# Turning the attention weights of a latent-attention stage with DVE squares and transfers within SBUF

## The chip, the cores and the metric

One core of a Trainium2 chip runs the whole program. The metric is device time in microseconds (us), as the median of the runs of one kernel. Engines: PE multiplies matrices, DVE and ACT work on vectors, POOL is hardly used here, and SP issues the transfers (DMA). SBUF is the on-chip memory of 128 partitions; PSUM holds the accumulators, eight banks of 128 x 512 f32.

## The reference

A decoder trunk of two layers on 256 tokens of width 2048, all f32. Layer 0 mixes by a gated MLP, layer 1 by latent attention with 12 heads; beside either, 4 heads attend to 256 memory tokens, and a gated feed-forward part follows. What matters here is the mixer of layer 1:

```
def mla_attention(q_lat, g_q_lat, w_uq, w_uk, w_uv, c_kv, k_rope, cos, sin):
    q = (rmsnorm(q_lat, g_q_lat) @ w_uq).reshape(B, S, MLA_HEADS, NOPE_DIM + ROPE_DIM)
    ...
        qa = jnp.einsum('bqhn,rhn->bqhr', qn, w_uk)
        s = (jnp.einsum('bqhr,bkr->bhqk', qa, c_kv)
             + jnp.einsum('bqhp,bkp->bhqk', qr, k_rope)).astype(jnp.float32) * scale
        s = jnp.where(k_pos[None, :] <= q_pos[:, None], s, -jnp.inf)
        p = jax.nn.softmax(s, axis=-1).astype(c_kv.dtype)
        o_lat = jnp.einsum('bhqk,bkr->bqhr', p, c_kv)
        return jnp.einsum('bqhr,rhv->bqhv', o_lat, w_uv)

def memory_attention(q_m, mem, g_mem, w_mem_kv):
    s = jnp.einsum('bshd,bmhd->bhsm', q, k).astype(jnp.float32) * (MEM_HEAD_DIM ** -0.5)
    p = jax.nn.softmax(s, axis=-1).astype(v.dtype)
    return jnp.einsum('bhsm,bmhd->bshd', p, v).reshape(B, S, MEM_W)

    # in the trunk, for layer 1
    x = x + jnp.concatenate([main, mo], axis=-1) @ w_out[l]
```

Softmax runs along the keys, and the sum over the keys that follows contracts them. On the chip a matmul contracts over partitions, so the weights p, which leave softmax with queries on partitions, must be turned before they can be used.

## The kernel before

All weights lie in HBM and are read once, in chunks of 128 x 1024 f32 (512 KB; 384 KB for the queries). `chunk` takes one of four `raw` buffers, issues the load on SP, and splits the chunk into two rounded parts: ACT copies it to `whi` (L110), DVE takes the difference to `wlo` (L111). A product then is three matmuls: high by high (L147), high by the low part of the activations (L148) and low by high (L150); in `gemm_tm`, with weights as the moving operand, these are L178 to L180. Activations are held as such pairs too, made by `split` (L232 on ACT, L233 on DVE).

The stage of layer 1 that matters (`layer_b`) computes the values in three chunks of 512 columns, `values(0)` to `values(2)`, into `scratch`; then for each of six pairs of heads `queries(i)` (two chunks of w_uq), `keys(i)` (one chunk of w_uk, expanded from the latent), and `scores(h)` for both heads: a matmul of kn and qn (L865) and two for the rotary part (L867), DVE's mask and maximum (L872, a custom operation), ACT's exponential with its sum (L877), DVE's reciprocal and scaling (L882). `turn(h)` transposes the three 128x128 blocks of a head's weights on PE (L889) and ACT copies them out of PSUM (L891). `attend(h)` multiplies by the values (L898, L899) and splits the result into `mainhl`. The four memory heads go the same way in `memory_scores` (L513; maximum L519, exponential L524, scaling L529), `memory_turn` (four transposes, L537, copied out by L541) and `memory_out` (L548). The loop over the pairs is written as a software pipeline: pair i's scores come one step after its queries, its turn and attend two steps after.

`w_out` is the output projection, 16 blocks of rows in chunks of two and in pairs of chunks, over eight such sweeps; the memory heads' rows come first. Its hooks run other work behind a given chunk of its first sweep.

Work of all engines is written in one program order; outside regions that fix it (`manual_schedule`) a scheduler reorders each engine's instructions by its own estimates, and each engine then takes its list in that order. A transfer issued by an engine waits in that engine's list until its source is ready, and all behind it waits too.

Later in the program, the feed-forward part has two operations that also occur in the change: DVE transposes of 32x32 squares (L968, `slot` from `xT`), and transfers within SBUF on SP in pieces of 32 elements (L973, `xt` from `slot`).

Of the kernel before, what the change touches and what calls it, by code (L numbers as in the profile page):

```python
# [8 lines left out]
F32 = mybir.dt.float32  # L9
# [3 lines left out]
AF = mybir.ActivationFunctionType  # L13
ALU = mybir.AluOpType
AX = mybir.AxisListType

P = 128
D = 2048
S = 256
NB = D // P  # L20
GH = 12
GW = GH * 128
MH = 4
# [45 lines left out]
    return out  # L69


class Kernel:
    def __init__(self, ctx, tc, t, out):
        self.tc, self.nc, self.t, self.out = tc, tc.nc, t, out
        self.ctx = ctx
        self.n = 0
        pool = lambda name, bufs=1, **k: ctx.enter_context(tc.tile_pool(name=name, bufs=bufs, **k))
# [16 lines left out]
    def chunk(self, src, nk, ncol, gains=None, twice=False, place=PLACE):  # L94
        nc, n = self.nc, nk * ncol
        raw = self.wp.tile([P, 1024], F32, tag="raw", name=self.uid("raw"), bufs=4)
        hi = self.wp.tile([P, 1088], F32R, tag="whi", name=self.uid("whi"), bufs=4)
        lo = self.wp.tile([P, 1088], F32R, tag="wlo", name=self.uid("wlo"), bufs=4)
        hi, lo = (x[:, place : place + 1024] for x in (hi, lo))
        view = lambda x: x[:, :n].rearrange("p (k c) -> p k c", k=nk)  # L100
        nc.sync.dma_start(out=view(raw), in_=src)
        if twice:
            both = hi[:, : 2 * n].rearrange("p (k o c) -> p k o c", o=2, c=ncol)
            for k in range(nk):
                r, h = view(raw)[:, k, :], both[:, k, 0, :]
                nc.scalar.activation(h, r, AF.Copy, scale=gains[k])
                nc.vector.scalar_tensor_tensor(both[:, k, 1, :], r, gains[k], h.bitcast(F32), ALU.mult, ALU.subtract)
            return hi[:, : 2 * n].rearrange("p (k c) -> p k c", k=nk)
        if gains is None:
            nc.scalar.activation(hi[:, :n], raw[:, :n], AF.Copy)  # L110
            nc.vector.tensor_tensor(lo[:, :n], raw[:, :n], hi[:, :n].bitcast(F32), ALU.subtract)  # L111
# [397 lines left out]
    def memory_scores(self, l, h, q, pool):  # L509
        nc = self.nc  # L510
        acc = self.psum()
        for sb in range(2):
            nc.tensor.matmul(  # L513
                acc[:, sb * S : (sb + 1) * S], q[:, sb * P : (sb + 1) * P], self.kT[l][:, h, :], start=True, stop=True
            )
        scale = 128 ** -0.5
        a3 = acc.rearrange("p (a m) -> p a m", a=2)
        mx = self.tmp(pool, [P, 2], "mx", 4)
        nc.vector.tensor_reduce(mx, a3, AX.X, ALU.max)  # L519
        nc.vector.tensor_scalar(mx, mx, -scale, None, ALU.mult)  # L520
        p = self.tmp(pool, [P, 2, S], "mp", 2)
        den = self.tmp(pool, [P, 2], "den", 4)
        for sb in range(2):
            nc.scalar.activation(  # L524
                p[:, sb, :], a3[:, sb, :], AF.Exp, bias=mx[:, sb : sb + 1], scale=scale, accum_out=den[:, sb : sb + 1]
            )
        nc.vector.reciprocal(den, den)
        for sb in range(2):
            nc.vector.tensor_scalar(p[:, sb, :], p[:, sb, :], den[:, sb : sb + 1], None, ALU.mult)  # L529
        return p  # L530

    def memory_turn(self, p, pool, bufs=2):
        nc = self.nc
        acc = self.psum()
        for mb in range(2):
            for sb in range(2):
                nc.tensor.transpose(  # L537
                    acc[:, mb * S + sb * P : mb * S + (sb + 1) * P], p[:, sb, mb * P : (mb + 1) * P], self.ident
                )
# [195 lines left out]
    def layer_b(self):  # L735
# [9 lines left out]
        with tc.tile_pool(name="lb", bufs=1) as lb:  # L745
# [103 lines left out]
            def keys(pr):  # L849
                kn[pr] = self.tmp(lp, [P, 2, S], "kn", 2)  # L850

                def ev(b, acc):
                    nc.scalar.activation(kn[pr][:, b : b + 2, :], acc, AF.Copy)

                self.gemm_fm(self.rows(wuk, pr * 256, 256), list(range(4)), 2, lambda k: chl[:, k, :], ev, nk=4)

            def scores(h):
                pr, j = divmod(h, 2)
                sc = self.psum()
                part = (slice(0, P), slice(P, 3 * P))  # L860
                for qb in range(2):
                    n = P * (qb + 1)
                    o = sc[:, part[qb]]
                    q = slice(qb * P, (qb + 1) * P)
                    mm(o, qn[pr][:, j, q], kn[pr][:, j, :n], start=True, stop=False)  # L865
# [4 lines left out]
                p = self.tmp(lp, [P, 3 * P], "p", 3)  # L870
                for qb in range(2):
                    nc.vector.tensor_tensor_reduce(  # L872
                        p[:, part[qb]], sc[:, part[qb]], self.mask[:, part[qb]], 1.0, -3e38, ALU.add, ALU.max, mx[:, qb : qb + 1]
                    )
                nc.vector.tensor_scalar(mx, mx, -scale, None, ALU.mult)
                for qb in range(2):
                    nc.scalar.activation(  # L877
                        p[:, part[qb]], p[:, part[qb]], AF.Exp, bias=mx[:, qb : qb + 1], scale=scale, accum_out=den[:, qb : qb + 1]
                    )
                nc.vector.reciprocal(den, den)  # L880
                for qb in range(2):
                    nc.vector.tensor_scalar(p[:, part[qb]], p[:, part[qb]], den[:, qb : qb + 1], None, ALU.mult)  # L882
                pa[h] = p

            def turn(h):
                p = pa.pop(h)
                acc = self.psum()
                for i in range(3):
                    nc.tensor.transpose(acc[:, i * P : (i + 1) * P], p[:, i * P : (i + 1) * P], self.ident)  # L889
                pT = self.tmp(lp, [P, 512], "pT", 3)  # L890
                nc.scalar.activation(pT[:, : 3 * P], acc[:, : 3 * P], AF.Copy)  # L891
                pa[h] = pT

            def attend(h):
                pT = pa.pop(h)
# [3 lines left out]
                mm(o[:, P:S], v[:, 1, cols], pT[:, S : S + P], start=False, stop=True)  # L899
                self.split(hl[:, h, :], o[:, :S])  # L900

            def mscores(h):
                pm[h] = self.memory_scores(1, h, qm[:, h, :], lp)

            def mturn(h):
                pm[h] = self.memory_turn(pm[h], lp, 3)

            def mout(h):
                self.memory_out(1, h, pm.pop(h), hl)

            n = GH // 2
            for i in range(n):
                queries(i)
                keys(i)
                if i >= 2:
                    turn(2 * i - 4)
                    turn(2 * i - 3)
                if i in (2, 4):
                    values(i // 2)
                if i >= 1:  # L920
                    scores(2 * i - 2)
                    scores(2 * i - 1)
                if i >= 2:
                    attend(2 * i - 4)
                    attend(2 * i - 3)
                if i < MH:
                    mscores(i)
                if 1 <= i <= MH:
                    mturn(i - 1)
                if 2 <= i <= MH + 1:  # L930
                    mout(i - 2)
            each = lambda f, *hs: [lambda h=h: f(h) for h in hs]
            for f in each(scores, 10, 11) + each(turn, 8, 9):
                f()
            hooks = {0: each(attend, 8, 9) + each(turn, 10, 11), 2: each(attend, 10, 11)}
            self.w_out(1, hl, [12, 13, 14, 15] + list(range(12)), hooks)
            ctx.close()

    def run(self):
# [146 lines left out]
```

## Time and profile before

| | |
|---|---|
| median of 3 runs | 2047.26 us (2047.03 to 2047.42) |
| the profiled execution | 2047.1 us |
| its span in the profile | 2045.4 us |
| granted PE clock | 0.999 |
| PE busy | 2035.9 us, 16232 instructions |
| DVE busy | 1359.1 us, 1859 instructions |
| ACT busy | 1043.5 us, 1345 instructions |
| weights and inputs read from HBM | 387.88 MB, 191 GB/s |

Times in the profile count from the start of the span. A group of instructions reads: line, engine, operation, output <- inputs, sizes, count, then total and mean duration, then the idle time of the engine ahead of it and what ended that. Matmuls are pipelined, so that the durations of neighbours overlap, and the cost of one is the distance to the next one's start.

### The profile page before, as it was taken

Reading aid. Unit: us, or ns where it says so; the run is one execution under the profiler, and the core shown is the slowest. Engines: PE = TensorE matmul, PEld = TensorE weight load, DVE = VectorE, ACT = ScalarE, POOL = GpSimd, SP = SyncE. Lnnn points to the kernel's source line nnn. Section 1 sums busy time; section 2 is a strip of 40 time slices with the busy share of each in tenths; the row PEclk is TensorE's granted clock in tenths of the full one; section 3 lists DMA queues with packets and bytes.
Section 4 is the critical chain, followed back from the end, with each engine's and each line's share of the span. In section 5 each row is a group of like instructions: output and inputs, shape, how many; then the busy total and the mean of one; then the engine's idle time right before and its main releaser. Section 6 shows DMA issues by size and latency. Waiting matters only on the chain.

```text
span 2045.4 us, 39005 instructions
## 1 busy us (share of the span) xinstructions
PE 2035.9 (100%) x16232; PEld 1969.4 (96%) x16232; DVE 1359.1 (66%) x1859; ACT 1043.5 (51%) x1345; POOL 94.5 (5%) x125
## 2 busy tenths in 40 slices
PE   9999999999999999999999999999999999999998
PEld 8989999999999999999999999999988999889997
DVE  6865667767556666557689875786655667656675
ACT  6754644555435554345555665455544455434553
POOL 0000013000000000000052001300000000000000
PEclk9999999999999999999999999999999999999999
DMA  8675465666666666666666644578766666666654
GB/s 309 188 230 175 155 197 188 196 196 188 203 189 193 199 191 198 190 196 192 189 196 177 179 129 154 183 209 219 225 196 194 189 198 193 194 196 188 196 185 155
DMA packets 219858, 394.62 MB, mean 193 GB/s; under 512 B 30880, under 2 KB 37408, under 8 KB 219552
## 3 DMA queue, kind: packets, MB, share of 16 engines
q1 hardware_dynamic: 219392, 391.60, 62.6%
q8 instruction: 127, 2.08, 0.4%
q10 hardware_dynamic: 288, 0.52, 0.1%
q14 instruction: 51, 0.42, 0.1%
HBM read 387.88 MB, written 2.10 MB: 191 GB/s over the span
## 4 chain that ended last, share of the span: by engine, by line
PE 99%; DMA 0%; issue 0%; DVE 0%; ACT 0%; POOLq 0%; POOL 0%
PE ps L150 26%; PE ps L147 26%; PE ps L148 26%; PE ps L178 6%; PE ps L180 6%; PE ps L179 6%; DMA raw<-in_w_mem_kv 0%; PE ps L865 0%; PE ps L548 0%; PE ps L513 0%; PE ps L485 0%; PE ps L484 0%; PE ps L487 0%; PE ps L688 0%; PE ps L898 0%; PE ps L867 0%
## 5 line engine op out<-in xcount | busy, mean ns | idle before, releaser
L111 DVE TENSOR_TENSOR wlo<-raw,whi 128x1024 fp32r<-128x1024 f32 (+1 forms) x672 | 818.6, 1235 | 612.9 <-issue 414.6
L110 ACT ACTIVATE whi<-raw 128x1024 fp32r<-128x1024 f32 (+1 forms) x672 | 705.2, 1056 | 794.1 <-PE ps L148 591.6
L147 PE MATMUL ps<-xhl,whi 128*128 128x256 f32 x3264 | 752.8, 277 | 0.0
L148 PE MATMUL ps<-xhl,whi 128*128 128x256 f32 x3264 | 750.8, 276 | 0.0
L148 PEld LDWEIGHTS ps<-xhl,whi 128*128 128x128 f32 x3264 | 612.8, 188 | 0.4
L147 PEld LDWEIGHTS ps<-xhl,whi 128*128 128x128 f32 x3264 | 612.6, 188 | 0.4
L150 PE MATMUL ps<-xhl,wlo 128*128 128x256 f32 x3264 | 403.2, 276 | 0.0
L150 PEld LDWEIGHTS ps<-xhl,wlo 128*128 128x128 f32 x3264 | 385.1, 188 | 0.0
L147 PE MATMUL ps<-h,whi 128*128 128x256 f32 x704 | 161.6, 276 | 0.0
L148 PE MATMUL ps<-h,whi 128*128 128x256 f32 x704 | 161.5, 276 | 0.0
L603 DVE SCALAR_TENSOR_TENSOR c<-a,cT,c 128x255 f32<-128x255 f32 (+1 forms) x352 | 146.3, 478 | 0.0
L179 PE MATMUL ps<-wlo,h 128*128 128x512 f32 (+1 forms) x364 | 139.0, 382 | 0.0
L180 PE MATMUL ps<-whi,h 128*128 128x512 f32 (+1 forms) x364 | 138.7, 382 | 0.0
L178 PE MATMUL ps<-whi,h 128*128 128x512 f32 (+1 forms) x364 | 138.3, 382 | 0.0
L148 PEld LDWEIGHTS ps<-h,whi 128*128 128x128 f32 x704 | 131.9, 188 | 0.0
L147 PEld LDWEIGHTS ps<-h,whi 128*128 128x128 f32 x704 | 131.9, 188 | 0.0
L600 ACT ACTIVATE c<-a,cT 128x256 f32<-128x256 f32 x176 | 91.6, 591 | 76.5 <-DVE a L228 76.5
L147 PE MATMUL ps<-mainhl,whi 128*128 128x256 f32 x512 | 118.0, 277 | 0.0
L148 PE MATMUL ps<-mainhl,whi 128*128 128x256 f32 x512 | 117.9, 276 | 0.0
L148 PEld LDWEIGHTS ps<-mainhl,whi 128*128 128x128 f32 x512 | 96.1, 188 | 0.0
L147 PEld LDWEIGHTS ps<-mainhl,whi 128*128 128x128 f32 x512 | 96.1, 188 | 0.0
L150 PE MATMUL ps<-h,wlo 128*128 128x256 f32 x704 | 86.9, 276 | 0.0
(246 smaller groups left out, 1972.2 us busy)
## 6 DMA issues: line engine op xcount, KB each, us to landing
raw<-in_w_ffn_up SPq DMA_DIRECT2D x352, 512.0 KB, 4.3
raw<-in_w_ffn_down SPq DMA_DIRECT2D x176, 512.0 KB, 4.6
raw<-in_w_out SPq DMA_DIRECT2D x64, 512.0 KB, 4.8
raw<-in_w_in_a SPq DMA_DIRECT2D x56, 512.0 KB, 4.4
raw<-in_w_mem_kv SPq DMA_DIRECT2D x30, 512.0 KB, 5.6
raw<-in_w_in_b SPq DMA_DIRECT2D x16, 512.0 KB, 4.1
raw<-in_w_uq SPq DMA_DIRECT2D x12, 384.0 KB, 3.4
raw<-in_w_kv_a SPq DMA_DIRECT2D x8, 512.0 KB, 4.3
```

Source lines behind the costliest of these rows:

```text
L110: nc.scalar.activation(hi[:, :n], raw[:, :n], AF.Copy)
L111: nc.vector.tensor_tensor(lo[:, :n], raw[:, :n], hi[:, :n].bitcast(F32), ALU.subtract)
L147: mm(acc, wh, x[:, :S], start=first, stop=False)
L148: mm(acc, wh, x[:, S:], start=False, stop=False)
L150: mm(acc, wl, x[:, :S], start=False, stop=last)
L178: mm(acc, xh, wh, start=first, stop=False)
L179: mm(acc, xh, wl, start=False, stop=False)
L180: mm(acc, xl, wh, start=False, stop=last)
L600: nc.scalar.activation(c[:, i, :], a[:, i, :], AF.Identity, scale=w(2), bias=w(3))
L603: nc.vector.scalar_tensor_tensor(o, a[:, i, : S - 2 + j], w(j), o, ALU.mult, ALU.add)
```

## The change

In layer 1 the weights p are no longer turned on PE.

- Softmax's last scaling is done by ACT (a copy with a scale per partition) in place of DVE.
- All heads of a batch write their weights into one wide buffer: `pm` for the four memory heads, a part of `scratch` for heads 0 to 5, `room` for heads 6 to 11.
- `Turn.squares` lets DVE transpose the 32x32 squares of that buffer into a small one, regrouped so that each band of 32 columns is together. There are 2 such operations of 128 x 1024 for the memory heads and 3 of 128 x 768 for either batch of heads, 8 in all.
- `Turn.place` moves one band of 32 partitions from the small buffer to another band of the wide one, by a transfer on SP. 16 places complete a turn, 48 in all. The memory heads' places have 32 x 16 pieces of 32 elements, the others 32 x 18.
- The places are not issued where they are written: `ask` puts them in a list, and `chunk` takes the next entry off it right after a weight load (`some`), so that a stated number of places follows each load.
- Within the stage PE and SP now run in program order, and the order is another: memory scores are early; `values(1)` follows keys(3); the four memory outputs, the attends of heads 0 to 5 and `values(2)` follow scores(11); the attends of heads 6 to 11 follow the third chunk of `w_out`.

```diff
+class Pending(list):
+    def some(self):
+        for f in self.pop(0) if self else ():
+            f()
+
+    def ask(self, steps, counts):
+        for n in counts:
+            self.append(steps[:n])
+            steps = steps[n:]
...
         nc.sync.dma_start(out=view(raw), in_=src)
+        self.pending.some()
...
         for sb in range(2):
-            nc.vector.tensor_scalar(p[:, sb, :], p[:, sb, :], den[:, sb : sb + 1], None, ALU.mult)
+            if by_act:
+                nc.scalar.activation(p[:, sb], p[:, sb], AF.Copy, scale=den[:, sb : sb + 1])
+            else:
+                nc.vector.tensor_scalar(p[:, sb], p[:, sb], den[:, sb : sb + 1], None, ALU.mult)
...
+                def squares(self, first, count):
+                    src = self.p[:, first * P : (first + count) * P].rearrange("p (n b c) -> p n b c", n=count, b=4)
+                    dst = self.small[:, :, first : first + count, :].rearrange("p b n c -> p n b c")
+                    nc.vector.transpose(dst, src)
+
+                def place(self, q, b):
+                    out = self.p[lanes(b), : self.n * P].rearrange("p (n q c) -> p n q c", n=self.n, q=4)[:, :, q, :]
+                    nc.sync.dma_start(out=out, in_=self.small[lanes(q), b])
...
                 for qb in range(2):
-                    nc.vector.tensor_scalar(p[:, part[qb]], p[:, part[qb]], den[:, qb : qb + 1], None, ALU.mult)
-                pa[h] = p
-
-            def turn(h):
-                p = pa.pop(h)
-                acc = self.psum()
-                for i in range(3):
-                    nc.tensor.transpose(acc[:, i * P : (i + 1) * P], p[:, i * P : (i + 1) * P], self.ident)
-                pT = self.tmp(lp, [P, 512], "pT", 3)
-                nc.scalar.activation(pT[:, : 3 * P], acc[:, : 3 * P], AF.Copy)
-                pa[h] = pT
+                    nc.scalar.activation(p[:, part[qb]], p[:, part[qb]], AF.Copy, scale=den[:, qb : qb + 1])
...
+            with tc.manual_schedule(engines={mybir.EngineType.SP, mybir.EngineType.PE}):
+                for i in range(GH // 2):
+                    if i == 3:
+                        memory.ask(0, 0, 6, 5, 5)
+                    if i == 5:
+                        turns[0].ask(0, 0, 16)
+                    for f in (queries, keys) if i else (keys, mscores, queries):
+                        f(i)
+                    if i == 2:
+                        each(lambda j: memory.squares(8 * j, 8), *range(2))
+                    if i == 4:
+                        each(lambda j: turns[0].squares(6 * j, 6), *range(3))
+                    if i == 3:
+                        values(1)
+                    if i >= 1:
+                        each(scores, 2 * i - 2, 2 * i - 1)
+                    each(mscores, *((1,), (2, 3), (), (), (), ())[i])
+                turns[1].squares(0, 6)
+                each(scores, 10, 11)
+                each(mout, *range(MH))
+                turns[1].squares(6, 6)
+                each(attend, *range(GH // 2))
+                turns[1].squares(12, 6)
+                values(2)
+                turns[1].ask(0, 6, 6, 4)
+                self.w_out(1, hl, [12, 13, 14, 15] + list(range(12)), {2: [lambda: each(attend, *range(GH // 2, GH))]})
```

The orders below list an engine's instructions as line, operation, output <- inputs and sizes; a number behind a name tells buffers of one kind apart. SP around the second third of the values, before (raw_13708 to raw_13771 are queries(3) and keys(3)):

```order
L101 DMA raw_13708<-in_w_uq 128x2x384
L101 DMA raw_13732<-in_w_uq 128x2x384
L101 DMA raw_13771<-in_w_uk 128x4x256
L101 DMA raw_13816<-in_w_uv 128x2x512
L101 DMA raw_13834<-in_w_uv 128x2x512
L101 DMA raw_13927<-in_w_uq 128x2x384
```

And SP at the two chunks of `values(1)` after, behind queries(3) and keys(3):

```order
L114 DMA raw_13857<-in_w_uq 128x2x384
L114 DMA raw_13881<-in_w_uq 128x2x384
L114 DMA raw_13920<-in_w_uk 128x4x256
L893 DMA pm<-room 32x16x32 x6
L114 DMA raw_13959<-in_w_uv 128x2x512
L893 DMA pm<-room 32x16x32 x5
L114 DMA raw_13982<-in_w_uv 128x2x512
L893 DMA pm<-room 32x16x32 x5
L114 DMA raw_14043<-in_w_uq 128x2x384
```

Six places now stand ahead of the first w_uv chunk, five more ahead of the second. What they wait for stands on DVE after, where ps_13821 and ps_13838 are the scores of heads 2 and 3 and the square is the second of the memory heads':

```order
L913 ISA scratch,mx_13828<-ps_13821,mask 128x128
L913 ISA mx_13828 128x1
L913 ISA scratch,mx_13828<-ps_13821,mask 128x256
L913 ISA mx_13828 128x1
L913 ISA scratch,mx_13845<-ps_13838,mask 128x128
L913 ISA mx_13845 128x1
L913 ISA scratch,mx_13845<-ps_13838,mask 128x256
L913 ISA mx_13845 128x1
L889 STREAM_TRANSPOSE room<-pm 128x8x4x32
L916 TENSOR_SCALAR mx_13828<-mx_13828 128x2
```

The square is taken only when the masks and maxima of scores(2) and scores(3) are done. SP at the start of the output projection, before:

```order
L101 DMA raw_14521<-in_w_out 128x2x512
L101 DMA raw_14527<-in_w_out 128x2x512
L101 DMA raw_14603<-in_w_out 128x2x512
L101 DMA raw_14609<-in_w_out 128x2x512
L101 DMA raw_14673<-in_w_out 128x2x512
L101 DMA raw_14679<-in_w_out 128x2x512
```

And after, from the places of heads 0 to 5 (scratch<-scratch) and `values(2)` on:

```order
L893 DMA scratch<-scratch 32x18x32 x16
L114 DMA raw_14409<-in_w_uv 128x2x512
L114 DMA raw_14427<-in_w_uv 128x2x512
L114 DMA raw_14451<-in_w_out 128x2x512
L114 DMA raw_14457<-in_w_out 128x2x512
L893 DMA room<-scratch 32x18x32 x6
L114 DMA raw_14517<-in_w_out 128x2x512
L893 DMA room<-scratch 32x18x32 x6
L114 DMA raw_14529<-in_w_out 128x2x512
L893 DMA room<-scratch 32x18x32 x4
L114 DMA raw_14617<-in_w_out 128x2x512
```

The places of heads 6 to 11 (room<-scratch) stand ahead of the third, fourth and fifth chunk of w_out. In all, PE has 52 matmul instructions fewer, DVE 24 instructions fewer, ACT 16 more, and SP 48 transfers more.

More of the change, by code (lines that the diff above doesn't have):

```diff
@@ L69, in two_pi_pieces @@
     return out
+class Pending(list):
[6 more added lines that the diff above has]
+            steps = steps[n:]
+        assert not steps
 class Kernel:
@@ L908, in mout @@
             def mout(h):
[L909 to L936, printed above, removed]
+                self.memory_out(1, h, pm[:, 512 * h : 512 * (h + 1)], hl)
+            turns = [batch(k) for k in range(2)]
+            each = lambda f, *hs: [f(h) for h in hs]
+            with tc.manual_schedule(engines={mybir.EngineType.SP, mybir.EngineType.PE}):
[24 more added lines that the diff above has]
+                self.w_out(1, hl, [12, 13, 14, 15] + list(range(12)), {2: [lambda: each(attend, *range(GH // 2, GH))]})
```

41 lines of the change are left out of this document (29 added, 12 removed).

## Prediction

> **What bounds the kernel now.** I read the page first, then who waits for whom on PE, then the stage that the change rewrites.
>
> ```profile
> span 2045.4 us, 39005 instructions
> PE 2035.9 (100%) x16232; PEld 1969.4 (96%) x16232; DVE 1359.1 (66%) x1859; ACT 1043.5 (51%) x1345; POOL 94.5 (5%) x125
> PE 99%; DMA 0%; issue 0%; DVE 0%; ACT 0%; POOLq 0%; POOL 0%
> PE ps L288 <- DVE ones L279: 1.1, 1, 1.1
> PE ps L147 <- ACT whi L132: 0.4, 1, 0.4
> ```
>
> The first lines are the page's: PE is busy for the whole span and makes up 99% of the chain that ended last. The last two are the full list of PE's waits: 1.5 us, all at the start. So this kernel is the list of its matmuls: a matmul that goes is worth its own time, and a wait that comes in is paid in full. The stage in question runs from the first queries to the third chunk pair of the output projection:
>
> ```profile
> 1144.91:1247.45 102.54, 102.54 (x782) 98.28 (x781) 73.79 (x207) 70.71 (x158) 0.10 (x1) 1.00 0.46 135
> ```
>
> (Columns: length, busy PE, weight loads, DVE, ACT, POOL, granted clock, DMA share, GB/s.) 102.54 of 102.54 us is matmul; DVE and ACT have about 30 us to spare each, but spread thin.
>
> **What the change removes.** PE loses 36 transposes of attention weights (12 heads x 3) and 16 of memory weights (4 heads x 4), 52 in all.
>
> ```profile
> 1143.09 0.39 PE L179 MATMUL ps<-wlo,chl 128*128 128x512 f32 x1
> ...
> 1144.67 0.40 PE L180 MATMUL ps<-whi,chl 128*128 128x512 f32 x1
> ...
> 1183.36 0.84 PE L150 MATMUL ps<-qhl,wlo 128*128 128x256 f32 x6
> ...
> 1185.40 0.84 PE L150 MATMUL ps<-qhl,wlo 128*128 128x256 f32 x6
> 1186.08 0.28 PE L147 MATMUL ps<-chl,whi 128*128 128x256 f32 x1
> ...
> 1188.81 0.82 PE L889 MATMUL ps<-ident,p 128*128 128x128 f32 x6
> 1189.46 0.39 PE L865 MATMUL ps<-kn,qn 128*128 128x128 f32 x2
> ...
> 1191.69 0.59 PE L898 MATMUL ps<-pT,scratch 128*128 128x256 f32 x2
> ...
> 1193.00 1.03 PE L513 MATMUL ps<-kT,qm 128*128 128x256 f32 x4
> 1193.86 0.60 PE L537 MATMUL ps<-ident,mp 128*128 128x128 f32 x4
> ...
> 1245.63 1.98 PE L150 MATMUL ps<-mainhl,wlo 128*128 128x256 f32 x16
> ...
> 1251.08 1.98 PE L150 MATMUL ps<-mainhl,wlo 128*128 128x256 f32 x16
> ```
>
> Matmuls overlap, so the cost is the distance between starts: six transposes take 1189.46 - 1188.81 = 0.65 us, 0.108 each. 52 x 0.108 = **-5.6 us**. The same rows give the other lengths on PE: a chunk of queries 1185.40 - 1183.36 = 2.04, two of them 4.08; keys 1188.81 - 1186.08 = 2.73; two heads of scores 1191.69 - 1189.46 = 2.23; two attends 1193.00 - 1191.69 = 1.31; a head of memory scores 1193.86 - 1193.00 = 0.86, and as much for a memory output, which has the same four matmuls; a chunk pair of the output projection 1251.08 - 1245.63 = 5.45; a matmul of values (1144.67 - 1143.09) / 7 = 0.226, and 24 of them 5.4. The evictions that go with the transposes, and the scaling that moves from DVE to ACT, cost nothing by themselves: no wait of PE names either engine here.
>
> **What it adds.** Eight 32x32 square transposes on DVE and 48 transfers within SBUF, called places, on SP, the queue that also loads every weight. The nearest rows are the square transposes and scattered transfers at the start of the feed-forward stage, and the weight loads:
>
> ```profile
> L973 SPq DMA_DIRECT2D xt<-slot x16: 597/597/1913, 1365.5 to 1445.9; - x16
> L968 DVE STREAM_TRANSPOSE slot<-xT x4: 1237/1240/1242, 1336.9 to 1353.2; 128x1024 f32<-128x1024 f32 x4
> DMA to landing us min/median/max: 4.2/5.7/7.6
> L101 SPq DMA_DIRECT2D raw<-in_w_uv x6: 367/368/368, 1125.1 to 1179.2; - x6
> DMA to landing us min/median/max: 3.6/4.0/5.0
> DMA to landing us min/median/max: 3.8/4.8/7.2
> ```
>
> (The first landing line is that of xt<-slot, the second of the w_uv loads, the third of the w_out loads.) An xt<-slot transfer moves 32 partitions x 1024 elements in pieces of 32 elements, 1024 pieces, and holds SP for 0.597 us; a place has 512 or 576 such pieces. Between 0.37 (the issue of a weight load) and 0.60 I take 0.45, with the gap to the next 0.5 us; and a landing of 3.5 us, under the least of a transfer twice as large and next to the least of a weight load. The square over 128x1024 takes 1.24 us, over 128x768 0.93.
>
> Three places in SP's order decide whether PE still finds its weights in time. For each I run PE without waits from 1144.91 (below: +t), and see when the chunk it needs is split.
>
> ```profile
> L111 DVE TENSOR_TENSOR wlo<-raw,whi 128x1024 fp32r<-128x1024 f32 x20 | 24.2, 1223 | 17.3 <-issue 10.0 <-ACT whi L110 7.2
> L110 ACT ACTIVATE whi<-raw 128x1024 fp32r<-128x1024 f32 x21 | 22.3, 1061 | 18.9 <-PE ps L148 10.8 <-PE ps L180 6.0 <-ACT qn L841 2.0
> L872 DVE CUSTOM_DVE_ANT_0 p<-ps,mask 128x256 f32<-128x256 f32 x12 | 5.0, 420 | 0.0
> L877 ACT ACTIVATE p<-p,mx 128x256 f32<-128x256 f32 x12 | 6.0, 497 | 0.0
> L877 ACT ACTIVATE p<-p,mx 128x128 f32<-128x128 f32 x12 | 4.8, 397 | 6.7 <-DVE mx L875 6.7
> L232 ACT ACTIVATE mainhl<-ps 128x256 fp32r<-128x256 f32 x16 | 5.8, 375 | 4.8 <-PE ps L899 4.7
> ```
>
> A chunk's way after its issue: landing, 1.06 us of ACT (L110) to the first matmul, 1.22 of DVE (L111) to the second.
>
> 1. *Memory weights, before values(1).* By the new order of PE, up to the end of scores(3) PE does three queries (12.2), three keys (8.2), four heads of scores (4.5) and four of memory scores (3.4), which is +28.3. On DVE the second memory square stands behind the mask and maximum of scores(3), so it ends at +28.3 + 0.2 + 0.5 + 1.24 = +30.3. On SP the first six places wait for it, and the first w_uv chunk is behind them: issued +33.3, landed +37.3, split by ACT +38.4 and by DVE +39.6. PE is through with queries(3) and keys(3) at +35.1 and needs the low half 0.2 later. **Wait 4.4 us**, 3.3 of it without any matmul. Queued behind PE's waiting matmul is all its later work; nobody else gains by it. If the places cost SP nothing it is still 1.3; if they cost 0.6 each, 5.0. The second chunk, behind five more places (+2.5), is split about **0.5** after PE wants it.
> 2. *Heads 0 to 5.* Their squares are done by about +50, and sixteen places back to back have landed 8.0 + 3.5 = 11.5 us later, +61.5. Attend(0) is due at +66.6. Hidden, with 5 us of cover. What is not covered: batch 1's first square reuses the small buffer, so DVE stands until the last landing, and the evictions behind it hold PSUM banks that PE wants before values(2): **0.5** (0 to 0.9).
> 3. *Heads 6 to 11, within the output projection.* After scores(11) ACT has three high halves of weights (3.2), six evictions of outputs (2.3), four exponentials with their accumulators (2.6) and six scalings taken at the exponentials' 0.45 (2.7); the last square ends about 11.2 us after PE leaves scores(11). PE meanwhile has four memory outputs (3.4), six attends (3.9), values(2) (5.4) and one chunk pair (5.45), 18.2, +0.5 by the wait above. The third chunk is behind six places: 11.2 + 3.0 + a landing of 4.0 to 4.8 + 1.06 = 19.3 to 20.1 against 18.7; the fourth, behind six more, is late again by 1.5 or so. I take **2.3** together, from 0 (landings at 3.6, squares 1 us earlier) to 4. The attends of heads 6 to 11 come a pair later and find their places landed.
>
> Sum: -5.6 + 4.4 + 0.5 + 0.5 + 2.3 = **+2.1 us**. The profiled execution took 2047.1 us (span 2045.4 and 1.7 around it), the median is 2047.26: I forecast **2049.2**. The measurement can tell about 0.2%, 4.1 us, from no change, so this reads as the same.
>
> **Rivals.**
> - *The loads are hidden anyway.* Then the 5.6 us are won and the time is 2041.5. For it: weights are usually ahead here (PE waits for none of them after the start). Against it: four `raw` buffers can only run ahead as far as SP does, and SP stands at a place whose square cannot exist before scores(3) has ended. It needs the first w_uv chunk about 4 us earlier. To be faster by over 4.1 us all waits together must stay under 1.5, which the 1.3 of place 1 alone nearly uses up. 0.10.
> - *The places drain more slowly than SP issues them* (slower). A place writes scattered pieces; one xt<-slot issue took 1913 ns where most took 597, so SP can be held back by what is in flight. 23 places lie ahead of late chunks or late squares (6 + 5 + 6 + 6), so each 0.1 us more per place costs 2.3 us: at 0.75 the time is 2049.2 + 5.8 = 2055, and at 1.0 also place 2 loses its cover (16 landed at +69.5 against +66.6, and the squares behind it by about as much), some 2049.2 + 11.5 + 6 = 2067. It decides from 0.6 us per place, which is the row of a transfer twice as large. 0.22. [...] No row here shows the rate of a burst.
> - *The waits let the clock down* (slower). Each of the two places has PE idle for 1 to 4 us.
>
> ```profile
> 0.00:4.00 4.00, 2.88 (x13) 2.88 (x14) 0.17 (x1) 1.28 (x1) 1.95 (x11) 1.00 0.46 138
> 2038.00:2042.00 4.00, 0.00 (x0) 0.00 (x0) 1.84 (x6) 1.33 (x2) 0.55 (x1) 1.00 0.82 321
> 2042.00:2045.40 3.40, 0.00 (x0) 0.00 (x0) 0.00 (x0) 0.00 (x0) 0.00 (x0) 0.50 0.46 170
> ```
>
>   The last two rows: at the end of the kernel the granted clock holds at 1.00 through 4 us without a matmul and is 0.50 after. The first: at the cold start 13 small matmuls took 2.88 us, 0.22 each, against 0.108 for the transposes of the same size, so a cold spell cost 13 x 0.11 = 1.5 us. Two of them: 2049.2 + 3.0 = 2052.2. It decides from about 4 us of idle, where I expect 3.3. 0.13. [...]
>
> **How the numbers follow.** The likeliest case has 0.55 and its own range 2046 to 2051; the first rival 0.10 (faster), the second 0.22 and the third 0.13 (slower). Faster 0.10, same 0.55, slower 0.35. The range leaves out most of the first rival and the part of the second above 0.85 us per place: 2044 to 2058.
>
> **What the profile after would show.** Right: no transposes in this stage; among PE's waits one of 3 to 5 us in front of values(1), released by ACT's or DVE's half of a w_uv chunk, and one or two of 1 to 2 us at the second chunk pair of w_out; SP waiting for the squares; places of 0.4 to 0.5 us; attends 0 to 5 without a wait; granted clock 1.00. Wrong: no wait before values(1) (first rival); places of over 0.6 us, or attends waiting for their landing (second); matmuls of 0.22 us after a wait (third). A wait at a place that I have not named, for instance of queries on an eviction that the longer ACT queue holds up, would make it wrong as well.

## The result, and the profile after

| | before | after |
|---|---|---|
| median | 2047.22 us (2047.03 to 2047.44, 6 runs) | 2061.30 us (2060.95 to 2062.83, 6 runs) |
| span of the profiled execution | 2045.4 us | 2059.9 us |
| ratio | | 1.007 [1.0059, 1.0081] |

The change costs 14.1 us, where 2 were forecast, within a range that ended at 2058. The page of the kernel after, and the full list of PE's waits behind it (line numbers are now those of the changed code: L161, L162, L164 are the three matmuls of a chunk, L192 to L194 those with weights as the moving operand, L124 and L125 the halves of the weights):

```profile
span 2059.9 us, 38931 instructions
PE 2036.6 (99%) x16180; PEld 1968.1 (96%) x16180; DVE 1357.7 (66%) x1835; ACT 1047.0 (51%) x1361; POOL 94.5 (5%) x125
PE 95%; SPq 2%; DMA 1%; ACT 1%; DVE 1%; issue 0%; POOLq 0%; POOL 0%; ACTq 0%
PE ps L192 <- ACT whi L124: 5.8, 1, 5.8
PE ps L161 <- ACT whi L124: 5.2, 2, 3.2
PE ps L192 <- DVE mainhl L247: 1.6, 1, 1.6
PE ps L302 <- DVE ones L293: 1.1, 1, 1.1
PE ps L161 <- ACT whi L146: 0.9, 1, 0.9
PE ps L193 <- DVE wlo L125: 0.5, 1, 0.5
PE ps L929 <- DVE mainhl L247: 0.2, 1, 0.2
```

PE has 52 instructions fewer and yet no less busy time, and SP's queue now has 2% of the chain. All waits that are new stand where the forecast had put them: 5.8 + 0.5 us before values(1), 5.2 us (2.0 and 3.2) at the third and fourth chunk of w_out, 1.6 + 0.2 us before values(2). The stage by windows (columns: length, busy PE, weight loads, DVE, ACT, POOL, granted clock, DMA share, GB/s): the whole of it, then the stretch behind the wait before values(1) and two behind that at w_out:

```profile
1146.00:1262.04 116.04, 102.73 (x730) 96.81 (x728) 72.86 (x186) 74.87 (x175) 0.10 (x1) 0.96 0.62 150
1187.50:1192.70 5.20, 4.66 (x10) 3.37 (x11) 2.45 (x2) 1.08 (x2) 0.00 (x0) 0.51 1.10 198
1247.40:1249.00 1.60, 1.59 (x7) 1.59 (x8) 1.22 (x1) 0.00 (x0) 0.00 (x0) 0.50 0.96 246
1249.00:1251.00 2.00, 2.00 (x13) 2.00 (x12) 0.00 (x0) 0.86 (x1) 0.00 (x0) 0.60 1.05 399
```

The stage takes 116.04 us instead of 102.54, 13.5 more, which is all but 1 us of the difference of the spans (the stage begins at 1146.0 instead of 1144.9, and that varies between kernels that are the same up to there: 1144.7 in one, 1145.8 in another below). Twice the granted clock is at half behind a wait (0.51 and 0.50), so that the busy time of PE grows although it has less to do.

SP at the first of the three places (start, length, then what was issued and how many), and DVE ahead of it:

```profile
1177.34 4.10 SPq L893 DMA_DIRECT2D pm<-room  x6
1181.49 0.62 SPq L114 DMA_DIRECT2D raw<-in_w_uv  x1
1182.15 3.55 SPq L893 DMA_DIRECT2D pm<-room  x5
1185.74 0.62 SPq L114 DMA_DIRECT2D raw<-in_w_uv  x1
```

```profile
1172.91 0.97 DVE L889 STREAM_TRANSPOSE scratch<-scratch 128x768 f32<-128x768 f32 x1
1173.81 1.18 DVE L125 TENSOR_TENSOR wlo<-raw,whi 128x1024 fp32r<-128x1024 f32 x1
1174.91 0.28 DVE L913 CUSTOM_DVE_ANT_0 scratch<-ps,mask 128x128 f32<-128x128 f32 x1
...
1176.02 1.24 DVE L889 STREAM_TRANSPOSE room<-pm 128x1024 f32<-128x1024 f32 x1
```

```profile
1187.58 0.80 PE L192 MATMUL ps<-whi,chl 128*128 128x512 f32 x1 [5.80 <-ACT whi L124]
1188.84 0.80 PE L193 MATMUL ps<-wlo,chl 128*128 128x512 f32 x1 [0.47 <-DVE wlo L125]
```

The square of the memory heads ends at 1177.26, six places hold SP for 4.15 us (0.69 apart), the w_uv load goes out at 1181.49, lands 5.0 us later, and PE starts values(1) at 1187.58. The matmul durations of 0.80 us, against 0.40 before, go with the half clock (0.51).

The transfers themselves (duration of the issue, least, median and most), and the landings of w_uv loads, before 3.6/4.0/5.0:

```profile
L893 SPq DMA_DIRECT2D pm<-room x16: 592/628/839, 1177.3 to 1189.1; - x16
L893 SPq DMA_DIRECT2D scratch<-scratch x16: 597/632/1521, 1206.9 to 1217.9; - x16
L893 SPq DMA_DIRECT2D room<-scratch x16: 591/632/1042, 1231.9 to 1244.0; - x16
DMA to landing us min/median/max: 4.1/4.7/5.0
```

### The profile page after: what moved, and what is told of

The parts are those of the page before. It is cut to its first block, busy times and chain, and to the rows that moved or that the text cites. A ratio compares the mean times of both kernels' runs of the same rounds, so it can differ in the third digit from the quotient of the medians.

```text
span 2059.9 us, 38931 instructions
## 1 busy us (share of the span) xinstructions
PE 2036.6 (99%) x16180; PEld 1968.1 (96%) x16180; DVE 1357.7 (66%) x1835; ACT 1047.0 (51%) x1361; POOL 94.5 (5%) x125
## 4 chain that ended last, share of the span: by engine, by line
PE 95%; SPq 2%; DMA 1%; ACT 1%; DVE 1%; issue 0%; POOLq 0%; POOL 0%; ACTq 0%
PE ps L164 25%; PE ps L161 25%; PE ps L162 25%; PE ps L192 5%; PE ps L193 5%; PE ps L194 5%; SPq L893 1%; DMA raw<-in_w_mem_kv 1%; ACT whi L124 0%; PE ps L499 0%; PE ps L498 0%; PE ps L501 0%; PE ps L527 0%; PE ps L705 0%; DMA raw<-in_w_uq 0%
## 5 line engine op out<-in xcount | busy, mean ns | idle before, releaser
L125 DVE TENSOR_TENSOR wlo<-raw,whi 128x1024 fp32r<-128x1024 f32 (+1 forms) x672 | 818.9, 1235 | 627.6 <-issue 424.2
L124 ACT ACTIVATE whi<-raw 128x1024 fp32r<-128x1024 f32 (+1 forms) x672 | 705.0, 1056 | 804.4 <-PE ps L162 589.4
L161 PE MATMUL ps<-xhl,whi 128*128 128x256 f32 x3264 | 752.8, 277 | 0.0
L162 PE MATMUL ps<-xhl,whi 128*128 128x256 f32 x3264 | 750.7, 276 | 0.0
L161 PEld LDWEIGHTS ps<-xhl,whi 128*128 128x128 f32 x3264 | 612.6, 188 | 0.4
L162 PEld LDWEIGHTS ps<-xhl,whi 128*128 128x128 f32 x3264 | 612.6, 188 | 0.4
L164 PE MATMUL ps<-xhl,wlo 128*128 128x256 f32 x3264 | 403.2, 276 | 0.0
L164 PEld LDWEIGHTS ps<-xhl,wlo 128*128 128x128 f32 x3264 | 385.1, 188 | 0.0
L161 PE MATMUL ps<-h,whi 128*128 128x256 f32 x704 | 161.6, 276 | 0.0
L162 PE MATMUL ps<-h,whi 128*128 128x256 f32 x704 | 161.5, 276 | 0.0
L194 PE MATMUL ps<-whi,h 128*128 128x512 f32 (+1 forms) x364 | 138.7, 382 | 0.0
L192 PE MATMUL ps<-whi,h 128*128 128x512 f32 (+1 forms) x364 | 138.3, 382 | 0.0
L161 PEld LDWEIGHTS ps<-h,whi 128*128 128x128 f32 x704 | 131.9, 188 | 0.0
L162 PEld LDWEIGHTS ps<-h,whi 128*128 128x128 f32 x704 | 131.9, 188 | 0.0
L161 PE MATMUL ps<-mainhl,whi 128*128 128x256 f32 x512 | 119.5, 279 | 5.2 <-ACT whi L124 5.2
L162 PE MATMUL ps<-mainhl,whi 128*128 128x256 f32 x512 | 119.0, 278 | 0.0
L161 PEld LDWEIGHTS ps<-mainhl,whi 128*128 128x128 f32 x512 | 97.2, 190 | 5.6 <-ACT whi L124 5.6
L162 PEld LDWEIGHTS ps<-mainhl,whi 128*128 128x128 f32 x512 | 97.1, 190 | 0.0
L164 PE MATMUL ps<-h,wlo 128*128 128x256 f32 x704 | 86.9, 276 | 0.0
```

Source lines behind the costliest of these rows:

```text
L161: mm(acc, wh, x[:, :S], start=first, stop=False)
L162: mm(acc, wh, x[:, S:], start=False, stop=False)
L164: mm(acc, wl, x[:, :S], start=False, stop=last)
L192: mm(acc, xh, wh, start=first, stop=False)
L194: mm(acc, xl, wh, start=False, stop=last)
```

## The experiments

Two theories. *Queue order*: PE waits because weight loads stand on SP behind places at about 0.675 us each; put the places behind the loads, and the waits go. *Traffic*: what the places move holds the loads up, wherever they stand. Each kernel below is the one after with the edit shown; its short name stands behind the title. Only PE and SP keep the written order in this stage. DVE's and ACT's lists are the scheduler's, and in the traces they come out in another order in each kernel. So a wait of a microsecond that comes or goes beside those that an edit aims at is not shown to be the edit's own work.

**Memory places behind the loads of values(1).** (mem_late)

```diff
-                        memory.ask(0, 0, 6, 5, 5)
+                        memory.ask(0, 0, 0, 0, 4, 4, 4, 4)
```

> The memory heads' sixteen places are asked for 4 at a time behind the loads that follow both w_uv chunks of values(1), instead of 6, 5 and 5 around them. Theory (queue order): the w_uv chunk came late because it stood on SP behind places at 0.675 us each; PE's wait of 5.8 + 0.5 us before values(1) and the 2.4 us of half-speed matmuls after it go: 2061.3 - 8.7 = 2052.6, and no wait over 1 us at queries(4). Rival (traffic): the places slow the loads by what they move, wherever they stand, so the loads of queries(4) are late instead: 2058 or more.

2054.78 us (2052.74 to 2055.35), ratio to before 1.0034 [1.0021, 1.0047]. The waits before values(1) are gone, and keys(4), behind eight places, wait only 0.3 us. Of the 8.7 us 6.5 came back by the medians (8.3 in the profiled executions). A wait of 1.0 us for an eviction by ACT at scores(10) is new; the 1.9 us before values(2) have given way to 1.4 us at an attend, and at w_out the waits are 2.9 and 2.4 us instead of 2.0 and 3.2. What the rest of the shortfall is made of is not shown.

**Places of heads 6 to 11 behind the fourth w_out load.** (out_late)

```diff
-                turns[1].ask(0, 6, 6, 4)
+                turns[1].ask(0, 0, 0, 16)
```

> The sixteen places of heads 6 to 11 are asked for in one go behind the fourth w_out load, instead of 6, 6 and 4 behind the second, third and fourth. Theory (queue order): the waits of 2.0 and 3.2 us at the second chunk pair of w_out and 1.9 us of half-speed matmuls go; a new wait of 0 to 1.5 us for the last landings before attends 6 to 11, or for the fifth chunk: 2061.3 - 7.1 + (0 to 1.5) = 2054.2 to 2055.7. Rival (traffic): the loss only moves to the fifth and sixth chunk: 2059 or more.

2054.47 us (2053.59 to 2057.33), 1.0039 [1.0025, 1.0053]. No wait at w_out is left, none for landings came.

**Both.** (both_late)

> Both edits together (memory places 4 at a time behind the loads after values(1); places of heads 6 to 11 all behind the fourth w_out load). Theory: the gains add up, 2061.3 - 8.7 - 6.4 = 2046 (2045 to 2048), level with the kernel before, since the wait before values(2) and the slower matmuls of the stage stay. Rival (traffic): 2056 or more.

2046.95 us (2046.21 to 2048.22, 10 runs), 1.0000 [0.9990, 1.0009]. All of the loss against the kernel before is undone by the order of the same transfers, and the gains add up (6.5 and 6.8 us alone, 14.4 together). PE's waits in the stage:

```profile
PE ps L929 <- DVE mainhl L247: 1.4, 1, 1.4
PE ps L906 <- ACT kn L870: 1.0, 1, 1.0
PE ps L929 <- DMA room<-scratch: 0.7, 1, 0.7
PE ps L161 <- ACT whi L124: 0.4, 1, 0.4
```

They hold 3.5 of the 5.6 us that the transposes were worth.

**No places at all.** (no_places) The 48 transfers are left out, so the attends multiply weights of which only the squares are turned.

> The kernel after without its 48 places (the attends then multiply weights of which only the squares are turned). Theory: the places on SP are the whole loss; without them the 5.6 us of transposes are won, less some 1 us for matmuls at 0.120 in place of 0.1135 us and less a wait of about 1 us for ACT at scores(10): 2047.2 - 3.6 = 2043.6 (2042 to 2045). Rival: the squares on DVE and the scalings on ACT cost as much by themselves, then waits stay and the time is 2047 or more.

2043.92 us (2043.40 to 2044.52, 10 runs), 0.9985 [0.9976, 0.9994]. The places are worth 17.4 us of the time after; beside them the squares on DVE, the scalings on ACT and the new order cost one wait of 1.3 us (at scores(10), for the rotary query). The saving is there, and the transfers take it.

**Places by POOL.** (by_pool)

```diff
-                    nc.sync.dma_start(out=out, in_=self.small[lanes(q), b])
+                    nc.gpsimd.dma_start(out=out, in_=self.small[lanes(q), b])
```

> The kernel after with its places issued by POOL, whose queue has nothing else to do in this stage, in place of SP; numbers of places and bytes are the same. Theory (queue order): no weight load stands behind a place, so PE's waits before values(1) and at the second chunk pair of w_out go, with the half-speed matmuls behind them: 2061.3 - 8.7 - 7.1 = 2045.5 as long as POOL issues a place in about 1 us; if it takes longer, attends wait for landings instead (POOL's price is not known). Rival (traffic): the loads are late as before, 2058 or more.

2049.82 us (2048.01 to 2051.63, 10 runs), 1.0013 [1.0004, 1.0022]. The same bytes, and PE waits for no weight load: the order on SP's queue is what made it wait. The traffic is felt all the same. Between 1170 and 1215 the loads land after 6.9 us in the median, where the kernel before has 3.8, but SP issues them early enough for that (landings of the loads in by_pool, then before):

```profile
DMA to landing us min/median/max: 3.1/6.9/9.8
DMA to landing us min/median/max: 3.2/3.8/4.9
```

But the attends now wait for landings, and the clock falls behind that wait too (window of 2 us just after it):

```profile
PE ps L929 <- DMA scratch<-scratch: 2.9, 1, 2.9
L893 POOL DMA_DIRECT2D scratch<-scratch x16: 667/667/677, 1196.9 to 1212.5; - x16
1219.00:1221.00 2.00, 2.00 (x8) 1.73 (x8) 1.73 (x4) 0.38 (x1) 0.22 (x1) 0.50 0.00 0
```

**Each place as two halves.** (halves)

```diff
-                    nc.sync.dma_start(out=out, in_=self.small[lanes(q), b])
+                    h = self.n // 2
+                    for s in (slice(0, h), slice(h, self.n)):
+                        nc.sync.dma_start(out=out[:, s], in_=self.small[lanes(q), b, s])
```

> The kernel after with each place issued as two transfers of half the pieces (32x8x32 or 32x9x32), 96 in all, two for one wherever a place stood. If SP's 0.63 us is the price of a transfer, six places' worth ahead of a chunk takes 8 us in place of 4: waits of 9 to 10 us before values(1), twice 4 us more at w_out and a late values(2), 2075 to 2085. If it is a price per piece, a half costs 0.3 and the time stays at 2061 (2060 to 2063).

2078.06 us (one run). A transfer of half the pieces holds SP about as long as a whole one, 609 to 612 ns in the median against 628 to 632; here the price is one per transfer:

```profile
L895 SPq DMA_DIRECT2D pm<-room x32: 585/609/1366, 1162.5 to 1197.9; - x32
L895 SPq DMA_DIRECT2D scratch<-scratch x32: 591/611/1412, 1206.4 to 1235.1; - x32
L895 SPq DMA_DIRECT2D room<-scratch x32: 585/612/952, 1238.4 to 1263.1; - x32
```

**Matmuls of a constant in the wait.** (warm) 36 of them between keys(3) and values(1):

```diff
                     if i == 3:
+                        spare = self.psum()
+                        for _ in range(36):
+                            nc.tensor.matmul(spare[:, :P], self.ones, self.ones, start=True, stop=True)
                         values(1)
```

> 36 matmuls of a constant (128x128, f32, 0.108 us each, 3.9 us) into a PSUM bank that nobody reads stand on PE between keys(3) and values(1), within the 5.8 us in which PE waits. Theory (clock): the half speed of the matmuls after the wait comes from the idle time; with some 2 us of it left the clock stays up and 2.4 us come back: 2058.9. Rival: the matmuls are slow because DMA writes contend with them (DMA share 0.99 there); then nothing changes, 2061.3.

2064.25 us (2063.26 to 2064.80), 1.0083 [1.0068, 1.0098]: 3 us more, not 2.4 less. The clock did what the theory says; a window behind the spot, with DMA as busy as before, has it at 1.00:

```profile
1190.00:1194.00 4.00, 3.10 (x13) 2.00 (x12) 1.22 (x1) 1.06 (x1) 0.00 (x0) 1.00 1.05 219
```

So at this spot the half speed comes with the idle time and not with the transfers: 1.00 at a DMA share of 1.05, where the kernel after has 0.51 at 1.10. The time did not follow for two reasons. Each of the 36 stands in the trace as two matmuls of 0.11 us (as the ten constant ones at the start of the program stand as x20), 7.96 us in all instead of 3.9, about 2 more than the wait that they were to fill. And with the clock up, values(1) still takes 7.2 us instead of 5.45, because now PE has to wait for the second chunk (0.75 us of idle at its low half); at half speed it had been slow enough not to. So values(1) ends 15.2 us after keys(3) and not 14.4. The rest, some 2 us, was lost at values(2) and w_out, and the windows show the clock there too (two of warm, then one of the kernel after):

```profile
1230.00:1234.00 4.00, 4.00 (x12) 3.12 (x11) 4.00 (x7) 2.74 (x8) 0.00 (x0) 0.57 0.02 3
1250.00:1254.00 4.00, 4.00 (x21) 4.00 (x20) 1.38 (x2) 2.11 (x2) 0.00 (x0) 0.50 1.04 383
1230.00:1234.00 4.00, 4.00 (x19) 3.32 (x18) 4.00 (x9) 2.61 (x6) 0.00 (x0) 1.00 0.16 27
```

In warm PE gets through 12 matmuls of values(2) in 4 us behind a wait of 1.6 us, where the kernel after, behind a wait of the same length, gets through 19; and behind w_out's wait of 3.2 us the clock is still at half at 1254, while the kernel after was back at full speed by 1251.

**Values(2) ahead of the memory outputs.** (values_first) Beside the two edits of both_late:

```diff
-                        turns[0].ask(0, 0, 16)
+                        turns[0].ask(0, 0, 0, 0, 16)
...
-                turns[1].squares(0, 6)
                 each(scores, 10, 11)
+                values(2)
+                turns[1].squares(0, 6)
                 each(mout, *range(MH))
                 turns[1].squares(6, 6)
                 each(attend, *range(GH // 2))
                 turns[1].squares(12, 6)
-                values(2)
```

> The order of both_late; besides, values(2) stands on PE ahead of the memory outputs and attends 0 to 5, the places of heads 0 to 5 behind both of its loads, and batch 1's first square behind it. Theory (queue order): no weight load of the stage stands behind a place that it needs not, so ACT's 2.1 us at the w_uv chunk and PE's 1.4 + 0.3 us go, and the landing before attend 6 (0.7) has more room: 2046.95 - 2.0 = 2045 (2044 to 2046). Rival: DVE's evictions of the memory outputs now stand behind squares and weight halves, PSUM banks run out: 2046.5 to 2049.

2047.82 us (2046.69 to 2049.33, 11 runs), 1.0003 [0.9994, 1.0012], in the rival's range. The wait for a bank before the attends is gone, but that for ACT's copy of the keys at scores(10) has grown from 1.0 to 1.8, and one of 0.6 is new. That is 2.4 us of waits instead of 3.5 in the profiled execution, the fastest of the eleven. What ate the gain is not the rival's mechanism: behind the wait of 1.8 us the clock falls, and matmuls that are not late run at half speed (the wait, then the spell behind it):

```profile
1207.20:1209.00 1.80, 0.01 (x2) 0.00 (x1) 1.67 (x8) 1.70 (x5) 0.00 (x0) 1.00 0.66 106
1210.50:1214.00 3.50, 3.50 (x12) 2.93 (x12) 2.03 (x9) 1.95 (x8) 0.00 (x0) 0.51 0.75 162
```

In 3.5 us at 0.51 of the clock about half of the work is left undone, an estimated 1.7 us. An earlier try with only the first line of this edit, all_late, had the attends of heads 0 to 5 in program order ahead of their places, so they read weights not yet placed, and the places waited for those reads; its 2066.79 us say nothing on the question, against this expectation:

> The order of both_late, and the sixteen places of heads 0 to 5 asked for behind both w_uv loads of values(2) instead of ahead of them. Theory (queue order): in both_late ACT stands 2.1 us for the w_uv chunk, behind 16 places, with the evictions of attends 0 to 5 queued behind it, and PE waits 1.4 + 0.3 us for a PSUM bank; with the loads first these go: 2046.95 - 1.7 = 2045.2 (2044.2 to 2046). Rival: DVE's wait for the landings before batch 1's first square holds the evictions; it stays, and the time with it: 2046.5 to 2047.5.

**The same order with places by POOL.** (pool_values_first) The counts of after, values(2) moved as above.

> by_pool with the same order of values(2), memory outputs and attends, so that the landings of heads 0 to 5 have 5.4 us more. Theory: PE's wait of 2.9 us for them and some 2 us of half-speed matmuls go: 2049.8 - 4.5 = 2045.3 (2044 to 2047). Rival: the wait is taken by PSUM banks (evictions behind DVE's wait for the landings): 2048 or more.

2050.99 us (2048.07 to 2052.82), 1.0019 [1.0009, 1.0028]. The attends of heads 0 to 5 no longer wait, but those of heads 6 to 11 do, 4.5 us for landings. Neither theory had that.

**Half of the places by POOL, half by SP**, in the order of both_late (split_late) and in that of after (split_after):

```diff
-                    nc.sync.dma_start(out=out, in_=self.small[lanes(q), b])
+                    (nc.gpsimd if b % 2 else nc.sync).dma_start(out=out, in_=self.small[lanes(q), b])
```

> The order of both_late, with half of the places of every turn (odd target bands) issued by POOL and half by SP, so that SP pays for 24 places in place of 48. Theory (price per transfer on a queue): a batch is issued in 5.4 us instead of 10.8, values(2)'s loads come 5.4 us earlier, and PE's 1.4 + 0.3 us for a PSUM bank and 0.7 for the landing go; the 1.0 us at scores(10), which is ACT's, stays: 2046.95 - 2.4 = 2044.6 (2044 to 2046). Rival: landings of POOL's transfers, 6 to 7 us under load in by_pool, make attends wait: 2047 to 2050.

> The kernel after with the same split over SP and POOL, counts as in after. Theory: three places instead of six ahead of a chunk: the wait before values(1) falls by 2.0 us, those at w_out by 2.0 and 2.0 with the half-speed spell behind them, and that before values(2): 2061.3 - 2 - 5.9 - 1.6 = 2051.8 (2049 to 2054). Rival (traffic): the same bytes, no change, 2058 or more.

2057.85 us (2056.75 to 2060.75), 1.0052 [1.0038, 1.0066], and 2065.98 us (2064.89 to 2066.77), 1.0091 [1.0077, 1.0105]. Both theories missed: with two queues the kernel is slower than with one. In split_late:

```profile
L893 SPq DMA_DIRECT2D scratch<-scratch x8: 597/1325/1986, 1203.1 to 1211.7; - x8
L893 POOL DMA_DIRECT2D scratch<-scratch x8: 665/665/674, 1203.8 to 1208.4; - x8
L893 SPq DMA_DIRECT2D room<-scratch x8: 592/1460/1743, 1231.4 to 1240.0; - x8
DMA to landing us min/median/max: 2.3/5.3/9.1
```

(The last line is that of all places; on SP alone, in the kernel after, 2.2/2.6/5.3.) Sixteen places still take from 1203.1 to 1213.3, when SP issues the next load: 0.63 each, hardly less than on SP alone (0.675), although each queue has only eight of them and SP issues no load in between. Beside POOL's places an issue on SP takes 1.3 and 1.5 us in the median of these two batches (0.63 on SP alone), and the loads behind places land later too (queries up to 9.1 us). I read this as a second limit beside the issue, the rate at which places drain: by these times one in about 0.63 us, which for 74 KB each is an estimated 117 GB/s. On one queue the two limits would then nearly coincide, and landings stay at 2.6 us in the median; with a second queue they take 5.3, a backlog. No run separates the two limits.

How much of the 11 us this backlog makes is not shown, because the list of DVE differs as well. In split_late the low half of a w_uv chunk of values(2) stands on DVE ahead of the masks of three heads. DVE stands for that chunk, PE stands at an attend for the masks behind it, and the clock falls after that:

```profile
1218.74 1.23 DVE L125 TENSOR_TENSOR wlo<-raw,whi 128x1024 fp32r<-128x1024 f32 x1 [8.01 <-ACT whi L124]
1220.65 0.70 PE L929 MATMUL ps<-scratch 128*128 128x256 f32 x2 [3.66 <-DVE mx L913]
```

The traffic theory thus was wrong as the account of the kernel after, but the traffic itself is felt in the landings of by_pool (6.9 us in the median for the loads, 3.8 before) and split_late (5.3 for the places, 2.6 in the kernel after).

## Why the prediction was wrong, step by step

The sum of the stage against the trace:

| term | forecast | measured | from |
|---|---|---|---|
| 52 transposes | -5.6 | -5.6 | no_places: its stage takes 99.08 us (1145.84 to 1244.92) instead of 102.54, 3.5 less, with a wait of 1.3 and 0.8 to 0.9 of slower matmuls in it |
| wait before values(1) | 4.4 | 6.3 | 5.80 + 0.47 |
| its second chunk | 0.5 | 0 | hidden by the half speed ahead of it |
| wait before values(2) | 0.5 | 1.9 | 1.64 + 0.22 |
| third and fourth w_out chunk | 2.3 | 5.2 | 1.99 + 3.20 |
| half clock | 0 | 4.3 | values(1) took 8.36 us with 0.47 of wait instead of 5.45: 2.4; the 32 matmuls with the high halves of chunks 3 and 4 took 8.73 with 3.20 of wait instead of 3.63: 1.9 |
| slower matmuls | 0 | 0.9 | about 200 at 0.120 us instead of about 80, last section |
| sum | +2.1 | +13.0 | stage +13.5 |

- *The step that failed first: the price of a place.* The prediction set it by its number of pieces, "Between 0.37 (the issue of a weight load) and 0.60 I take 0.45", 0.5 with the gap. In halves half the pieces still cost 0.61; a scattered transfer holds SP for 0.61 to 0.63 us in these kernels, 0.675 with the gap, which is the row of xt<-slot as it stood there (597). Scaling it down had no row behind it. Six places cost 4.15 us instead of 3.0. By size the largest term that the sum missed is another, the half clock: 4.3 us, put at nothing.
- *Two smaller misses in the same chain.* The w_uv load landed after 5.0 us, the largest of the three figures quoted, not the 4.0 of the median, with places in flight beside it (in by_pool, where places and loads overlap, loads land after 6.9 us in the median instead of 3.8); and the square came 1.0 us later than worked out, because DVE had the square of heads 0 and 1 and the low half of keys(3) ahead of the masks of scores(2). The order on DVE was read for what stands behind scores(3), and not for how late DVE itself already was. Of the 1.1, 1.0 and 1.0 us some 0.6 came off because PE was later too, and 0.6 because the first matmul ran at half speed, so that the second waited less: the difference of 1.9. (The 4.4 is 4.3 by the forecast's own terms, 39.6 less 35.1 and 0.2.)
- *At w_out* the same price comes twelve times: six places took 4.0 and then 4.6 us, where 3.0 was forecast. Both chunks landed 5.0 us after their issue (4.0 to 4.8 forecast), and the last square ended at 1231.9, 12.6 us after PE had left scores(11) at 1219.25. The forecast had 11.2 there; its own terms, 10.8 us of ACT and 0.93 of the square, add up to 11.7.
- *The clock.* The rival was there, priced at 3.0 for two spells (4.3 measured) and at 0.13, with "It decides from about 4 us of idle, where I expect 3.3". On that ground the sum put it at nothing. Both numbers failed: the wait was 5.8, and far shorter gaps do. In mem_late a gap of 2.9 us was enough:

```profile
1230.00:1234.00 4.00, 1.25 (x12) 1.05 (x10) 0.00 (x0) 0.94 (x1) 0.00 (x0) 1.00 1.26 200
1234.00:1237.00 3.00, 2.80 (x16) 2.50 (x16) 1.23 (x1) 0.12 (x1) 0.00 (x0) 0.72 0.94 218
1237.00:1239.40 2.40, 0.07 (x1) 0.07 (x1) 0.08 (x1) 1.06 (x1) 0.00 (x0) 0.50 1.30 151
```

  PE stands from 1231.2 to 1234.17, the clock still reads 1.00, and falls within the next 3 us, after PE is back. The mistake was to take the 4 us at the end of the kernel before, where the clock reads 1.00 too, as a lower bound for the gap: in these rows the clock follows late (1.00 up to 1234, 0.72 in the 3 us after), and a gap that has ended is still answered. Nor is 2.9 us a limit. A gap of 1.8 us did it in values_first, and one of 1.6 us in warm, with waits of 0.8 and 0.3 us shortly ahead of it, while gaps of 1.6 and 2.0 us in the kernel after did not. So the length of one gap does not settle it; what does stays open here. The row of the cold start that priced a spell also reads 1.00, although its matmuls take 0.22 us and the constant ones of warm 0.11, so the column can't be trusted that early.
- *Rivals taken as alternatives.* The second rival decides "from 0.6 us per place"; at 0.675 its own slope of 2.3 us per 0.1 gives 2049.2 + 4.0 = 2053.2, and the 4.3 of the third added to that 2057.5. They were given chances beside each other, but they belong together. At w_out the dearer places lengthen the waits, and the second of them (3.2 us) lets the clock down. Before values(1) the forecast's own gap of 3.3 us was longer than those that halved the clock in other kernels, so there the third was likely even at the forecast price of a place.
- *Right:* the value of the transposes; each of the three places, its releaser, and that batch 0's landings are hidden (no wait for one in the kernel after), as are those of heads 6 to 11.

## What to carry to other kernels

Where one queue loads the weights, price each small transfer by its issue (0.61 to 0.63 us here, with 256 pieces as with 576), and count how many stand ahead of the next load that a busy engine needs; then put them behind that load. Against the kernel without them, the same 48 transfers cost 17.4 us in one order and 3.0 in another; the saving on PE was 5.6, and the best order only came level with the kernel before. A wait of 2 to 3 us on PE can cost more than itself: behind waits of 1.8, 3.2 and 5.8 us matmuls ran at 0.51 to 0.56 of the clock for 3.5, 3.6 and 5.2 us; look at the granted clock behind every wait, also behind short ones. And before work is spread over a second queue, check that the first is limited by its issue alone.

## What was not expected of the hardware

- Gaps of 1.6 and 1.8 us on PE let the clock down in two kernels, and gaps of 1.6 and 2.0 us in a third did not; after the gap of 2.9 us in mem_late it falls when PE is already back (0.72, then 0.50).
- A weight load issued right behind a place takes 0.62 us to issue instead of 0.37 (lines of SP above).
- Two queues issuing such transfers together got hardly more through than one: 16 places in 10.1 us, against 10.8 on SP alone in both_late.
- Between 1172 and 1215 in the kernel after, 1172 and 1206 in no_places, and 1164 and 1170 before, matmuls of queries and keys follow each other at 0.120 us instead of 0.113, at a granted clock of 1.00 (outside the spell at half): about 80 of 495 in the whole stage before, about 200 after, and as many without places. It cost 0.5 us before and 1.4 after. Neither the places (no_places has it too) nor the clock explain it; the cause stays open.
